# A gated-linear-attention block with a convolutional feed-forward: the down projection's matmuls walk their columns in another order in each block product

## The chip, the cores and the metric

The kernel runs on one core of one Trainium2 chip. The metric is the device time of one execution in microseconds. The kernel before has a median of 2124.78 us over three runs (2121.08, 2124.78 and 2126.06).

## The reference

One transformer layer over 2048 tokens of width 1024 in float32: a token mixer (chunked gated linear attention with 4 heads), then a causal convolutional feed-forward. Each is modulated by a conditioning vector and closed with a residual and a layer norm. What the change touches is the last product of the feed-forward:

```python
def conv_ffn(h, w_up, conv_w, conv_b, w_down):
    u, g = jnp.split(h @ w_up, 2, axis=-1)
    u = lax.conv_general_dilated(u, conv_w[:, None, :], window_strides=(1,), padding=((CONV_W - 1, 0),), ...) + conv_b
    return (jax.nn.silu(u) * g) @ w_down

def post_norm_residual(x, cs, w_mod, b_mod, ln_gain, ln_bias, sublayer):
    shift, scale, gate = jnp.split((cs @ w_mod + b_mod)[:, None, :], 3, axis=-1)
    y = sublayer(x * (1 + scale) + shift)
    return layer_norm(DN_ALPHA * x + (1 + gate) * y, ln_gain, ln_bias)
```

The hidden width is 2816, so the down projection is (2048 x 2816) times (2816 x 1024).

## The kernel before, in words

**The large products.** A float32 product is made of three matmuls in a reduced float32 format. Each operand is split into a high part (a cast on ScalarE, L104) and a low part (what the cast lost, a subtraction on VectorE, L107). `mm3` (L109 to L112) then issues high by high, high by low and low by high, all into the same PSUM bank. The first operand is the stationary one, 128 x 128, loaded as weights; the second is the moving one, 128 partitions by 512 columns, and the sums of those 512 columns fill one bank of 512 float32 columns.

**The down projection (L1833 to the end).** It uses a scheme with seven block products instead of eight (Strassen-Winograd), on each half of the tokens, p = 0 and 1 (1024 tokens each). The seven combinations of hidden blocks lie in DRAM as `hc_d[p][i]`, the seven of weight blocks as `wc_d[i]`; each has NP = 11 slices of 128 rows. `ORDER = (0, 1, 4, 5, 6, 3, 2)` is the order in which the products i run. This makes 14 block products; the text numbers them 1 to 14 in order of time, so product 1 is p = 0, i = 0, and product 14 is p = 1, i = 2.

One product takes 4 tiles t of 128 tokens, and for each tile 11 slices: `mms(t, gi, got)` (L1953) calls `mm3` once or twice, because `groups` pairs the slices. The stationary operand is a 128-column piece of the hidden combination, the moving one a 512-column slice `w[:, 0, o:o + 512]` (high) or `w[:, 1, o:o + 512]` (low) of the weight combination. So a product has 4 x 11 x 3 = 132 matmuls of 512 columns.

**Banks.** The eight PSUM banks are two sets of four: "A" (`ps_mm`) and "C" (`ps_w`), one bank per tile t. `INTO` (L1938) says which set a product adds to. Products i = 0, 1 and 4 are `fresh`: they begin new sums; the others add to what stands in the set. After each product `evict` (L1962) lets VectorE add the banks to the rows of the result in SBUF (L1965). ScalarE, VectorE and GpSimd then do the last layer norm of a tile (`ln2`, `ln2_last`), and SyncE's queue stores it. Product 14 goes tile by tile, so that the last layer norms spread out.

**Supply.** `d_load` (L1851) issues the transfers of two slices from DRAM on SyncE's queue, up to four groups ahead; `d_split` (L1862) makes the high and low parts up to three groups ahead, in tiles named `dhl` or, every third time, `hl`. TensorE takes its matmuls in the order of the program; the scheduler of the language lets the first of them mix with the last products of the up projection.

Of the kernel before, what the change touches and what calls it, by code (L numbers as in the profile page):

```python
# [16 lines left out]
P = 128  # L17
# [21 lines left out]
def kernel(  # L39
# [43 lines left out]
    def psum(tag, bufs=1):  # L83
        return ps.tile([P, 512], F32, tag=tag, name="ps_" + tag, bufs=bufs)
# [24 lines left out]
    def mm3(po, a, b, first, last, resumed=False):  # L109
        nc.tensor.matmul(po, a[0], b[0], start=first, stop=False, skip_group_check=resumed)  # L110
        nc.tensor.matmul(po, a[0], b[1], start=False, stop=False, skip_group_check=resumed)  # L111
        return nc.tensor.matmul(po, a[1], b[0], start=False, stop=last, skip_group_check=resumed)  # L112
# [341 lines left out]
    if True:  # L454
# [86 lines left out]
        for n, (dk, more) in enumerate(PE_ROWS):  # L541
            wk = mod_row(start[0][0], dk)
            for c in range(4):
                i = nc.tensor.matmul(pm0[:, c:c + 1], wk[:, c // 2, c % 2 * P:c % 2 * P + P], cs[:, dk:dk + 1],
                                     start=n == 0 and c == 0, stop=False, skip_group_check=True)
# [1287 lines left out]
    ORDER = (0, 1, 4, 5, 6, 3, 2)  # L1833
# [11 lines left out]
        return hs  # L1845

    groups = [(p, i, g) for p in range(2) for i in ORDER for g in range(0, NP, 2)]
    flip = [0]
    dloaded, dready = [], []

# [23 lines left out]
    def d_get(q):  # L1874
        while len(dloaded) < min(q + 4, len(groups)):
            d_load()
        while len(dready) < min(q + 3, len(groups)):
            d_split()
        return dready[q]
# [12 lines left out]
    def ln2_last(p, b, t):  # L1892
        a, sm = acc.pop((p, b, t))
        st = sts.pop()
        nc.vector.bn_stats(st[:, 1], a[:, 512:1024])
        mv = smp.tile([P, 2], F32, tag="mv", name="mv")
        nc.vector.bn_aggr(mv, st)

        rs = smp.tile([P, 2], F32, tag="rs", name="rs")
        nc.scalar.activation(rs[:, 1:2], mv[:, 1:2], AF.Sqrt, bias=eps[:, 0:1])  # L1900
        ys = []
        for half in range(2):
            cs_ = slice(half * 512, half * 512 + 512)
            y = t2p.tile([P, 512], F32, tag="t2", name="y")
            i = nc.vector.scalar_tensor_tensor(y, a[:, cs_], mv[:, 0:1], rows[2][half], op0=ALU.subtract, op1=ALU.mult)
            if half == 0:
                order(nc.vector.reciprocal(rs[:, 0:1], rs[:, 1:2]), i)
            cut = (0, 256, 512) if t == 3 and half == 1 else (0, 512)
            for c0, c1 in zip(cut, cut[1:]):
                nc.vector.scalar_tensor_tensor(y[:, c0:c1], y[:, c0:c1], rs[:, 0:1], rows[3][half][:, c0:c1],  # L1910
                                               op0=ALU.mult, op1=ALU.add)
                store(outr[p * 8 + b * 4 + t][:, half * 512 + c0:half * 512 + c1], y[:, c0:c1])
# [31 lines left out]
    for p in range(2):  # L1944
        bank = {"A": [None] * 4, "C": [None] * 4}
        for i in ORDER:
            kind, b, half, whole = INTO[i]
            cs_ = slice(half * 512, half * 512 + 512)
            fresh = i in (0, 1, 4)
            ng = (NP + 1) // 2  # L1950
            outer = p == 1 and i == ORDER[-1]

            def mms(t, gi, got):  # L1953
                n = min(2, NP - 2 * gi)
                h, w = got
                for k in range(n):
                    o = k * 512
                    mm3(bank[kind][t], (h[:, 0, o + t * P:o + t * P + P], h[:, 1, o + t * P:o + t * P + P]),
                        (w[:, 0, o:o + 512], w[:, 1, o:o + 512]),
                        fresh and gi == 0 and k == 0, gi == ng - 1 and k == n - 1, not fresh)  # L1960

            def evict(t):  # L1962
                a, sm = acc[p, b, t]
                acc_out = {"accum_out": sm[:, half:half + 1]} if whole and not outer else {}
                nc.vector.scalar_tensor_tensor(a[:, cs_], bank[kind][t], 1.0, a[:, cs_],  # L1965
                                               op0=ALU.mult, op1=ALU.add, **acc_out)
                if outer:
                    ln2_last(p, b, t)
                elif i in (3, 2):
                    work.append((ln2, p, b, t))  # L1970

            if fresh:
                bank[kind] = [psum("mm" if kind == "A" else "w", 4) for t in range(4)]
            if i == 3 and p == 0:
                work += [(init_acc, 1, 0, t) for t in range(4)]
            if outer:
                nc.vector.memset(eps, EPS)
                got = [d_get(q + gi) for gi in range(ng)]
                for t in range(4):
                    sts.append(smp.tile([P, 2, 6], F32, tag="bst", name="bst"))  # L1980
                    nc.vector.bn_stats(sts[-1][:, 0], acc[p, b, t][0][:, 0:512])
                    for gi in range(ng):
                        mms(t, gi, got[gi])
                        if gi % 3 == 1 and work:
                            f, *a_ = work.pop(0)
                            f(*a_)
                    evict(t)
            else:
                for gi in range(ng):
                    got = d_get(q + gi)  # L1990
                    if work and (gi > 0 or work[0][0] is init_acc):
                        f, *a_ = work.pop(0)
                        f(*a_)
                    for t in range(4):
                        mms(t, gi, got)
                        if gi == ng - 1:
                            evict(t)
            q += ng
        work += [(init_acc, 1, 1, t) for t in range(4)] if p == 0 else []
# [58 lines left out]
```

## Time and profile before

| what | value |
|---|---|
| median of three runs | 2124.78 us |
| the profiled execution | 2121.6 us |
| its span, first to last instruction | 2119.9 us |
| mean granted TensorE clock | 0.996 |
| TensorE matmuls | 9381, 2085.8 us busy |
| ScalarE and VectorE busy | 1003.4 us and 1529.5 us |
| moved by DMA | 546.24 MB |

How to read it: the rows of the profile are times of one execution. PE is TensorE's matmul row, PEld its weight loads, DVE VectorE, ACT ScalarE, POOL GpSimd, SP SyncE. Matmuls are pipelined, and the length that is recorded for one reaches into the next, so the distance from start to start tells its price. A row of a group gives line, engine, operation, tiles (out<-in), shapes and count, then the busy time in us and the mean ns of one, then the idle time of the engine just before and what ended it. A row of a wait reads: who waited, for whom, us in total, times, the longest.

### The profile page before, as it was taken

The numbers are of one execution on the slowest core, as the hardware profiler recorded it, in microseconds if no ns is written. First come the engines' busy times: TensorE is split into PE (matmuls) and PEld (weight loads), VectorE is DVE, ScalarE is ACT, GpSimd is POOL, SyncE is SP. The second block draws the span as 40 slices with busy tenths as digits, with TensorE's granted clock in tenths as the row PEclk, the third lists the DMA queues.
The fourth block names the chain that finished last, engine by engine and source line by source line (L and its number), as shares of the span: only waits on it lengthen the run. The fifth ranks groups of instructions, "written<-read, shape, count | busy, mean of one in ns | idle before, by whom it ended". The sixth has DMA issues, their size and how long they took to land.

```text
span 2119.9 us, 26188 instructions
## 1 busy us (share of the span) xinstructions
PE 2085.8 (98%) x9381; PEld 1721.9 (81%) x9381; DVE 1529.5 (72%) x2022; ACT 1003.4 (47%) x1405; POOL 107.0 (5%) x254
## 2 busy tenths in 40 slices
PE   9999999999999998999999999999999999999998
PEld 7887887778888787888888888888888888888886
DVE  6855757776687667878777787666676796577557
ACT  4648636674555544644444454333333443344332
POOL 0000000001112201100000000000000000020001
PEclk9999999999999999999999999999999999999999
DMA  9787888788745885777756679877777897677562
GB/s 336 304 295 261 283 306 286 268 306 317 277 145 196 310 289 192 274 249 285 273 194 219 219 253 321 288 258 273 246 276 256 295 325 250 206 247 251 189 200 89
DMA packets 192035, 546.24 MB, mean 258 GB/s; under 512 B 24928, under 2 KB 33504, under 8 KB 186272
## 3 DMA queue, kind: packets, MB, share of 16 engines
q1 hardware_dynamic: 191904, 544.56, 73.5%
q8 instruction: 74, 1.21, 0.2%
q14 instruction: 57, 0.47, 0.1%
HBM read 357.58 MB, written 186.91 MB: 257 GB/s over the span
## 4 chain that ended last, share of the span: by engine, by line
PE 71%; DVE 3%; ACT 2%; DMA 2%; issue 1%; POOL 1%; SPq 0%; DVEq 0%; POOLq 0%; ACTq 0%
PE ps_mm L110 15%; PE ps_mm L112 15%; PE ps_mm L111 15%; PE ps_w L111 7%; PE ps_w L110 7%; PE ps_w L112 7%; PE ps_w L1326 1%; PE ps_w L1354 1%; PE ps_w L1356 1%; PE ps_w L1310 1%; DMA hl<-wf_d 1%; DMA A<-a_d 0%; PE ps_w L1375 0%; PE ps_w L1416 0%; ACT on L1369 0%
## 5 line engine op out<-in xcount | busy, mean ns | idle before, releaser
L110 PE MATMUL ps_mm<-xc,hl 128*128 128x512 f32 x920 | 361.8, 393 | 6.2 <-ACT u L448 4.5
L111 PE MATMUL ps_mm<-xc,hl 128*128 128x512 f32 x920 | 359.5, 391 | 0.0
L112 PE MATMUL ps_mm<-xc,hl 128*128 128x512 f32 x920 | 358.8, 391 | 0.0
L110 PEld LDWEIGHTS ps_mm<-xc,hl 128*128 128x128 f32 x920 | 173.5, 189 | 46.4 <-ACT u L448 6.6
L112 PEld LDWEIGHTS ps_mm<-xc,hl 128*128 128x128 f32 x920 | 173.4, 189 | 36.5 <-DVE hl L107 0.2
L111 PEld LDWEIGHTS ps_mm<-xc,hl 128*128 128x128 f32 x920 | 173.6, 189 | 36.1 <-issue 0.5
L110 PE MATMUL ps_w<-xc,hl 128*128 128x512 f32 x464 | 180.6, 389 | 0.0
L111 PE MATMUL ps_w<-xc,hl 128*128 128x512 f32 x464 | 180.5, 389 | 0.0
L112 PE MATMUL ps_w<-xc,hl 128*128 128x512 f32 x464 | 180.5, 389 | 0.0
L1655 DVE SCALAR_TENSOR_TENSOR ct<-U,cw_sb,ct 128x512 f32<-128x512 f32 x176 | 131.8, 749 | 22.8 <-ACT ct L1649 20.2
L104 ACT CAST hl<-wu 128x1024 fp32r<-128x1024 f32 x90 | 94.8, 1053 | 104.1 <-PE ps_mm L112 76.9
L448 ACT COPY u<-ps_mm 128x512 f32<-128x512 f32 x112 | 65.3, 583 | 159.4 <-PE ps_mm L112 152.0
L104 ACT CAST dhl<-raw 128x1024 fp32r<-128x1024 f32 x57 | 60.1, 1054 | 159.2 <-PE ps_mm L112 98.5
L107 DVE TENSOR_TENSOR hl<-wu,hl 128x1024 fp32r<-128x1024 f32 x90 | 110.0, 1222 | 30.2 <-ACT hl L104 29.9
L107 DVE TENSOR_TENSOR dhl<-raw,dhl 128x1024 fp32r<-128x1024 f32 x57 | 69.7, 1223 | 65.4 <-ACT dhl L104 65.4
L107 DVE TENSOR_TENSOR hl<-raw,hl 128x1024 fp32r<-128x1024 f32 (+1 forms) x63 | 69.3, 1104 | 56.1 <-ACT hl L104 55.8
L110 PE MATMUL ps_mm<-hl,xg 128*128 128x512 f32 x240 | 104.0, 433 | 3.6 <-DVE z L1526 3.6
L104 ACT CAST hl<-raw 128x1024 fp32r<-128x1024 f32 (+1 forms) x63 | 60.0, 955 | 99.4 <-PE ps_mm L112 42.1
L104 ACT CAST hl<-wg 128x1024 fp32r<-128x1024 f32 x56 | 59.0, 1053 | 97.6 <-PE ps_mm L112 85.0
L110 PE MATMUL ps_mm<-dhl 128*128 128x512 f32 x264 | 102.7, 389 | 0.0
L111 PE MATMUL ps_mm<-dhl 128*128 128x512 f32 x264 | 102.7, 389 | 0.0
L112 PE MATMUL ps_mm<-dhl 128*128 128x512 f32 x264 | 102.7, 389 | 0.0
(284 smaller groups left out, 4743.7 us busy)
## 6 DMA issues: line engine op xcount, KB each, us to landing
hc_d<-ct SPq DMA_DIRECT2D x154, 256.0 KB, 2.9
raw<-hc_d SPq DMA_DIRECT2D x70, 512.0 KB, 4.2
draw<-wc_d SPq DMA_DIRECT2D x70, 512.0 KB, 4.6
wu<-in_wup_dram SPq DMA_DIRECT2D x44, 512.0 KB, 5.3
wg<-in_wup_dram SPq DMA_DIRECT2D x44, 512.0 KB, 4.3
wh_d<-hl SPq DMA_DIRECT2D x22, 1024.0 KB, 4.8
hl<-wh_d SPq DMA_DIRECT2D x22, 1024.0 KB, 6.6
mraw<-in_mws_dram SPq DMA_DIRECT2D x40, 512.0 KB, 6.0
```

Of the source, the lines that this page charges most:

```text
L104: accs["copy"] = nc.scalar.copy(h, src)
L107: return nc.vector.tensor_tensor(l, src if lsrc is None else lsrc, h.bitcast(F32), op=ALU.subtract)
L110: nc.tensor.matmul(po, a[0], b[0], start=first, stop=False, skip_group_check=resumed)
L111: nc.tensor.matmul(po, a[0], b[1], start=False, stop=False, skip_group_check=resumed)
L112: return nc.tensor.matmul(po, a[1], b[0], start=False, stop=last, skip_group_check=resumed)
L448: return t, nc.scalar.copy(t, po)
L1310: nc.tensor.matmul(pav[:, i], KI[:, s * P:s * P + P], Q[:, s], start=True, stop=True)
L1326: nc.tensor.matmul(pst[:, s % 2 * DV:s % 2 * DV + DV], KTt[:, s * P:s * P + P], v[s], start=True, stop=True)
L1354: nc.tensor.matmul(pos_, at[:, i], v[s], start=True, stop=st is None)
L1356: nc.tensor.matmul(pos_, Q[:, s, 0:128], st, start=False, stop=True)
L1655: nc.vector.scalar_tensor_tensor(ct, U[:, o + i:o + i + 512], cw_sb[:, j, i:i + 1], ct, op0=ALU.mult, op1=ALU.add)
```

## The change

A table `WALK` gives each of the 14 block products an order in which its matmuls go through their 512 columns. An entry is (rows, run, down). With run = 0 the columns go from 0 to 511, or with down = 1 from 511 to 0. Otherwise the 512 columns are seen as `rows` equal parts, each cut into runs of `run` columns, and the walk takes the first run of each part, then the second of each part, and so on (with down = 1 from the last run to the first); inside a run the columns rise. The view is made once for the moving operand and once for the bank, so column c of the weights still ends in column c of the bank. The stationary operand, the evictions and the number of columns are unchanged; products 1 and 14 keep the order of before.

| product | p, i | columns |
|---|---|---|
| 1 and 14 | 0, 0 and 1, 2 | as before |
| 2 | 0, 1 | all 512 backwards |
| 3, 4 | 0, 4 and 0, 5 | 2 parts, runs of 16; 4 from the last run down |
| 5 | 0, 6 | 2 parts, runs of 32 |
| 6 | 0, 3 | 4 parts, runs of 16 |
| 7 | 0, 2 | runs of 16 from the last to the first |
| 8, 9, 10 | 1, 0, then 1, 1, then 1, 4 | 2 parts, runs of 8; of 64; of 4 |
| 11 | 1, 5 | 8 parts, runs of 16 |
| 12, 13 | 1, 6 and 1, 3 | 4 parts, runs of 32 and of 16, both down |

```diff
@@ -1845,6 +1845,8 @@
     groups = [(p, i, g) for p in range(2) for i in ORDER for g in range(0, NP, 2)]
+    WALK = ((1, 0, 0), (1, 0, 1), (2, 16, 0), (2, 16, 1), (2, 32, 0), (4, 16, 0), (1, 16, 1),
+            (2, 8, 0), (2, 64, 0), (2, 4, 0), (8, 16, 0), (4, 32, 1), (4, 16, 1), (1, 0, 0))
     flip = [0]
@@ -1947,6 +1949,15 @@
             fresh = i in (0, 1, 4)
+            rows_of, run, down = WALK[p * 7 + ORDER.index(i)]
+
+            def walk(a):
+                if run == 0:
+                    return a[:, ::-1] if down else a
+                v = a.rearrange("p (r c e) -> p c r e", r=rows_of, e=run)
+                v = v[:, ::-1] if down else v
+                return v[:, :, 0] if rows_of == 1 else v
+
             ng = (NP + 1) // 2
@@ -1955,8 +1966,8 @@
                 for k in range(n):
                     o = k * 512
-                    mm3(bank[kind][t], (h[:, 0, o + t * P:o + t * P + P], h[:, 1, o + t * P:o + t * P + P]),
-                        (w[:, 0, o:o + 512], w[:, 1, o:o + 512]),
+                    mm3(walk(bank[kind][t]), (h[:, 0, o + t * P:o + t * P + P], h[:, 1, o + t * P:o + t * P + P]),
+                        (walk(w[:, 0, o:o + 512]), walk(w[:, 1, o:o + 512])),
                         fresh and gi == 0 and k == 0, gi == ng - 1 and k == n - 1, not fresh)
```

## The prediction

> **What bounds the kernel now.** I read the page first, for which engine is full and which engine the chain that ended last runs through.
>
> ```profile
> span 2119.9 us, 26188 instructions
> ...
> PE 2085.8 (98%) x9381; PEld 1721.9 (81%) x9381; DVE 1529.5 (72%) x2022; ACT 1003.4 (47%) x1405; POOL 107.0 (5%) x254
> ...
> PE   9999999999999998999999999999999999999998
> ...
> PEclk9999999999999999999999999999999999999999
> ...
> PE 71%; DVE 3%; ACT 2%; DMA 2%; issue 1%; POOL 1%; SPq 0%; DVEq 0%; POOLq 0%; ACTq 0%
> ```
>
> TensorE is full in every slice, at a granted clock of nine tenths or more throughout, and the chain runs through it. A busy PE is not a PE at its peak, so next I cut out the down projection by time (busy time of each engine by stretch) and looked at its matmuls one by one (the timeline of PE; two rows of 28, without a break between them).
>
> ```profile
> core 0: us, PE busy (x) PEld busy (x) DVE busy (x) ACT busy (x) POOL busy (x), PEclk, DMA share, GB/s
> 1687.50:2111.50 424.00, 424.00 (x1872) 350.95 (x1871) 297.69 (x365) 167.60 (x191) 30.48 (x48) 1.00 0.67 225
> 2111.50:2119.90 8.40, 0.54 (x3) 0.12 (x1) 4.53 (x9) 0.29 (x1) 0.00 (x0) 0.72 0.24 90
> ```
>
> ```profile
> 1799.76 0.39 PE L110 MATMUL ps_mm<-dhl 128*128 128x512 f32 x1
> ...
> 1805.88 0.39 PE L110 MATMUL ps_mm<-dhl 128*128 128x512 f32 x1
> ```
>
> PE is busy for all 424.00 us of that stage, at clock 1.00. A matmul lasts 0.39 us in the record, but the next one starts sooner: 27 starts lie between the two rows, and (1805.88 - 1799.76) / 27 = 226.7 ns from start to start. That is the price of one matmul of 512 columns here, 226.7 / 512 = 0.443 ns a column; the 389 ns overlap with the neighbours. Check: 1872 x 226.7 ns = 424.4 us, the length of the stage. Nothing else sets the pace: weight loads, VectorE and ScalarE have room, and in the waits of this stage it is they who wait for PE:
>
> ```profile
> ACT dhl L104 <- PE ps_mm L112: 98.0, 29, 4.3
> ...
> ACT dhl L104 <- PE ps_w L112: 56.8, 17, 4.3
> ```
>
> So in this stage PE's own rate is the time. After it come 8.4 us of layer norm and stores, which the change does not touch.
>
> **How much the change reaches.** The groups of matmuls of this stage, one of three equal lines (L110; L111 and L112 have the same counts):
>
> ```profile
> L110 PE MATMUL ps_mm<-dhl 128*128 128x512 f32 x264 | 102.7, 389 | 0.0
> ...
> L110 PE MATMUL ps_w<-dhl 128*128 128x512 f32 x192 | 74.7, 389 | 0.0
> ...
> L110 PE MATMUL ps_mm<-hl 128*128 128x512 f32 x88 | 34.2, 389 | 0.0
> ...
> L110 PE MATMUL ps_w<-hl 128*128 128x512 f32 x72 | 28.0, 389 | 0.0
> ```
>
> 3 x (264 + 192 + 88 + 72) = 1848 matmuls, 132 for each of 14 block products, or 132 x 226.7 ns = 29.9 us a product. WALK leaves the first and the last product as they were; 12 x 132 = 1584 matmuls get another order. Product 2 (p = 0, i = 1) runs all 512 columns backwards. The other eleven walk forwards inside runs of 4 to 64 columns and jump between runs.
>
> What moves in the program: on PE, where the second product ends and the third (p = 0, i = 4) begins, before and then after. dhl and hl are the split operands, ps_w the bank.
>
> ```order
> L111 MATMUL ps_w<-hl 128x512
> L112 MATMUL ps_w<-hl 128x512
> L110 MATMUL ps_w<-dhl 128x512
> L111 MATMUL ps_w<-dhl 128x512
> L112 MATMUL ps_w<-dhl 128x512
> ```
>
> ```order
> L111 MATMUL ps_w<-hl 128x512
> L112 MATMUL ps_w<-hl 128x512
> L110 MATMUL ps_w<-dhl 128x16x2x16
> L111 MATMUL ps_w<-dhl 128x16x2x16
> L112 MATMUL ps_w<-dhl 128x16x2x16
> ```
>
> The same instructions in the same places; only the shape of the pattern differs: 16 steps, at each 2 runs of 16 columns. The backward product above it has one dimension as before, so its rows read alike. VectorE, ScalarE, GpSimd and SyncE keep every instruction and transfer in its place. One thing is added. On PE, where product 8 (p = 1, i = 0) begins, with the semaphores that each row waits for, before and then after:
>
> ```order
> L112 MATMUL ps_w<-hl 128x512
> L110 MATMUL ps_mm<-dhl 128x512 [waits Activation_49]
> L111 MATMUL ps_mm<-dhl 128x512 [waits DVE_49]
> L112 MATMUL ps_mm<-dhl 128x512
> L110 MATMUL ps_mm<-dhl 128x512
> ```
>
> ```order
> L112 MATMUL ps_w<-hl 128x32x16
> L110 MATMUL ps_mm<-dhl 128x32x2x8 [waits PE_49,Activation_49]
> L111 MATMUL ps_mm<-dhl 128x32x2x8 [waits DVE_49]
> L112 MATMUL ps_mm<-dhl 128x32x2x8
> L110 MATMUL ps_mm<-dhl 128x32x2x8
> ```
>
> The first matmul into each of the four banks waits for PE's own semaphore as well, in product 8 and again in product 9: eight waits.
>
> **The eight waits.** Each is for the earlier matmuls into the same bank. Those of product 8 wrote in product 6, those of product 9 in product 7, so a whole product (29.9 us) lies between and the wait is over before it starts: 0. Behind such a wait stands all of PE, and the casts of ScalarE behind that. Were each to hold PE until the matmul just before it has ended, it would cost what now overlaps, 389 - 227 = 162 ns, and eight of them 1.3 us. I take 0 and keep 1.3 us for the range.
>
> **The 1584 matmuls.** Nothing hides a slower matmul here, since PE has no idle time; each ns on all of them is 1.6 us of the end, in full. No matmul of this trace walks its columns in another order, so the price is bounded by the nearest rows.
>
> From above: there is a matmul that takes 512 columns at about half the pace, the plain-float32 one at L296, and one of 256 columns, L1326 (the chain of waits: start, length, what; then the groups by shape).
>
> ```profile
> 515.33 1.73 PE ps_w L1326 x8
> ...
> 1267.00 1.72 PE ps_w L296 x4
> ```
>
> ```profile
> L1326 PE MATMUL ps_w<-v,KTt 128*128 128x256 f32 x120 | 29.9, 379 | 0.0
> ...
> L296 PE MATMUL ps_w<-G,ones 128*128 128x512 f32 x8 | 3.8, 602 | 0.0
> ```
>
> 1.72 / 4 = 430 ns for 512 columns, 1.73 / 8 = 216 ns for 256. So half pace costs 430 - 227 = 203 ns more a matmul.
>
> From below: those two rows give (430 - 216) / 256 = 0.836 ns a column and 2 ns fixed. If our matmuls stream exactly twice as fast, 512 columns need 214 + 2 = 216 ns, and at most 11 ns a matmul could be won: 1584 x 11 ns = 17 us.
>
> What do broken patterns cost elsewhere? Row L562 casts and L565 subtracts 384 columns that are written in 24 runs of 16 with gaps between; the unbroken casts and subtractions of 512 and 1024 stand beside them (one tile's instructions; groups by shape).
>
> ```profile
> L562 ACT CAST waw<-war x1: 494/494/494, 20.1 to 20.1; 128x384 fp32r<-128x384 f32 x1
> L565 DVE TENSOR_TENSOR waw<-war,waw x1: 549/549/549, 25.3 to 25.3; 128x384 fp32r<-128x384 f32 x1
> ```
>
> ```profile
> L104 ACT CAST hl<-wu 128x1024 fp32r<-128x1024 f32 x90 | 94.8, 1053 | 104.1 <-PE ps_mm L112 76.9 <-DVE wu L352 12.0 <-PE ps_w L112 7.4
> ...
> L104 ACT CAST h<-s 128x512 fp32r<-128x512 f32 x34 | 20.8, 612 | 5.3 <-PE ps_mm L112 2.9 <-DVE s L352 2.5
> ```
>
> ```profile
> L107 DVE TENSOR_TENSOR hl<-wu,hl 128x1024 fp32r<-128x1024 f32 x90 | 110.0, 1222 | 30.2 <-ACT hl L104 29.9
> ...
> L107 DVE TENSOR_TENSOR h<-s,h 128x512 fp32r<-128x512 f32 x34 | 23.3, 686 | 13.4 <-ACT h L104 13.4
> ```
>
> ScalarE: (1053 - 612) / 512 = 0.861 ns a column, so 384 unbroken ones would take 612 - 128 x 0.861 = 502 ns; the broken ones took 494. VectorE: 1.047 ns a column, 686 - 134 = 552 ns; 549 measured. Twenty-four breaks cost nothing. Weakness: these engines move a column in 0.86 to 1.05 ns, PE in 0.44, so a break that fits under their pace may not fit under PE's. Still, the addresses come from the same kind of pattern, no row charges for a break, and I take 0 for PE too.
>
> The Trainium skill speaks on both sides. The Trainium skill's page "PSUM — Partial Sum Buffer", Specifications (TRN2), says of PSUM's 8-byte lines that any non-contiguous pattern slows matmuls significantly; by that sentence all 12 products lose, and with 203 ns each the sum would be 2443.2 us. The Trainium skill's page "Advanced Engine Details and Errata", Memory Cachelines, puts it as every two consecutive elements being contiguous for best throughput, and the two of a float32 pair stay neighbours in all fourteen orders, the backward one too; by that the sum stays. No row here shows a broken matmul, so neither is tested yet.
>
> The sum: 0 for 1584 matmuls, 0 for eight waits, nothing removed. The profiled execution took 2121.6 us (span 2119.9 and 1.7 around it), so 2121.6 stays; the median of the three runs is 2124.8, 3.2 above, and the runs lie from 2121.1 to 2126.1. I predict the median, 2124.8. About 0.2%, 4.2 us, is what a measurement of this kernel can tell from no change.
>
> **The rivals.** Each price is added to 2124.8.
>
> 1. Slower: only going backwards costs. If PE fetches or writes columns in pairs, rising ones, product 2 falls to half pace while runs of 4 or more keep theirs. 132 x 203 ns = 26.8 us: 2151.6. For it: 0.443 ns a column against 0.836 shows that the fast pace is twice another one that this PE has, so something could switch. Against it: nothing in the trace depends on direction. It decides the sign from 4.2 / 132 = 32 ns a matmul on.
> 2. Slower: each jump costs. The eleven broken products make 413 jumps for one matmul each (31 for each of the six with runs of 16, 15 for each of the two with 32, 63 with 8, 7 with 64, 127 with 4), 132 x 413 = 54,516 in all. At one column's time, 0.443 ns, 24.1 us: 2148.9; at two, 2173.1. Against it: the broken rows of ScalarE and VectorE.
> 3. Slower: every changed order runs at half pace. 1584 x 203 ns = 321.6 us: 2446.4. For it: no cover anywhere. Against it: the same rows. The rule of the Trainium skill's page "PSUM — Partial Sum Buffer" (Specifications) is this case; no row here shows it.
> 4. Faster: the remainder of 11 ns goes, at most 17 us: 2107.8. Nothing in the trace ties it to the order of columns.
>
> That the change does less than it says (a pattern folded back into a plain one) cannot be for the eleven, whose shapes stand in the order; for the backward one it would give the forecast's time.
>
> **How the numbers follow.** No effect: 0.64. Backwards alone: 0.14. Jumps: 0.07. Half pace throughout: 0.11. Faster: 0.04. So faster 0.04, within 0.2% 0.64, slower 0.32. The likeliest case alone spans 2119 to 2130, from the spread of the runs and the 1.3 us of waits. To hold 8 in 10 the range goes up to backwards alone with the spread above it, 2155, which takes in half of the jumps too (0.64 + 0.14 + 0.03); half pace and the dear jumps stay outside.
>
> **What would show it.** In the timeline of PE after the change: product 2 starts at 1722.9 us, as the first matmul into ps_w from dhl does now,
>
> ```profile
> L110 PE MATMUL ps_w<-dhl x192: 389/389/389, 1722.9 to 2110.5; 128*128 128x512 f32 x192
> ```
>
> and then one product each 29.9 us. Right: 226.7 ns from start to start in every product, and the stage still 424 us. Wrong: product 2 alone at some 430 ns (rival 1), the excess growing with the jumps and greatest in product 10 with runs of 4 (rival 2), 430 ns in twelve products (rival 3), or idle time at the start of products 8 and 9 (the waits).

## The result: 12.75 us slower

| | before | after |
|---|---|---|
| median of three runs | 2124.78 us | 2137.53 us |
| their lowest and highest | 2121.08 and 2126.06 | 2136.89 and 2138.75 |
| span of the profiled execution | 2119.9 us | 2135.7 us |
| stage of the down projection | 424.00 us | 440.80 us |

The ratio is 1.0060, with a 95% interval of 1.0039 to 1.0081: 8 to 17 us slower. That is inside the range, but it isn't the case that was called likeliest (no effect). The spans of the profiled executions differ by more, 15.8 us, because the one of before ran 3.2 us under its median. The page of the kernel after:

```profile
span 2135.7 us, 26190 instructions
...
PE 2105.2 (99%) x9381; PEld 1727.1 (81%) x9381; DVE 1530.1 (72%) x2022; ACT 1002.7 (47%) x1405; POOL 107.4 (5%) x254
...
PEclk9999999999999999999999999999999999999999
```

The counts of matmuls, casts and subtractions are those of before, and so is the clock. PE is busy 19.4 us longer and its weight loads 5.2; the other engines stay within 0.7. The two stretches that the prediction cut out (busy time by stretch, same columns):

```profile
core 0: us, PE busy (x) PEld busy (x) DVE busy (x) ACT busy (x) POOL busy (x), PEclk, DMA share, GB/s
1686.90:2127.70 440.80, 440.80 (x1873) 352.86 (x1871) 298.50 (x365) 167.66 (x191) 30.50 (x48) 1.00 0.64 217
2127.70:2135.70 8.00, 0.21 (x1) 0.00 (x0) 4.52 (x9) 0.29 (x1) 0.00 (x0) 0.75 0.19 69
```

The stage is 16.8 us longer and PE is busy for all of it at clock 1.00. It began 0.6 us earlier and the tail is 0.4 us shorter, which leaves the 15.8 us of the span. So the time came from matmuls that follow each other more slowly, not from a wait or a throttled clock. The first matmul of products 2 to 14 and the last one of product 14, from the timeline of PE (start, length, then the instruction):

```profile
1722.36 0.40 PE L110 MATMUL ps_w<-dhl 128*128 128x512 f32 x1
1753.16 0.41 PE L110 MATMUL ps_w<-dhl 128*128 128x512 f32 x1
1784.85 0.40 PE L110 MATMUL ps_mm<-dhl 128*128 128x512 f32 x1
1815.65 0.40 PE L110 MATMUL ps_mm<-dhl 128*128 128x512 f32 x1
1846.88 0.40 PE L110 MATMUL ps_mm<-dhl 128*128 128x512 f32 x1
1877.42 0.40 PE L110 MATMUL ps_w<-dhl 128*128 128x512 f32 x1
1908.22 0.41 PE L110 MATMUL ps_mm<-dhl 128*128 128x512 f32 x1
1940.34 0.40 PE L110 MATMUL ps_w<-dhl 128*128 128x512 f32 x1
1970.29 0.41 PE L110 MATMUL ps_w<-dhl 128*128 128x512 f32 x1
2003.30 0.41 PE L110 MATMUL ps_mm<-dhl 128*128 128x512 f32 x1
2034.92 0.40 PE L110 MATMUL ps_mm<-dhl 128*128 128x512 f32 x1
2066.16 0.40 PE L110 MATMUL ps_mm<-dhl 128*128 128x512 f32 x1
2097.79 0.39 PE L110 MATMUL ps_w<-dhl 128*128 128x512 f32 x1
...
2127.52 0.39 PE L112 MATMUL ps_w<-hl 128*128 128x512 f32 x1
```

The distance of two neighbouring rows divided by 132 (131 for product 14) is the pace of a product, the mean distance from one start to the next. In the table, a jump is a step from the end of one run to a run that isn't its neighbour above, and the excess is over the 226.7 ns of before.

| product | order | ns a matmul | excess, ns | jumps | excess per jump, ns |
|---|---|---|---|---|---|
| 2 | all backwards | 233.3 | 6.7 | none | |
| 3 | 2 parts, runs of 16 | 240.0 | 13.3 | 31 | 0.43 |
| 4 | the same, down | 233.3 | 6.7 | 31 | 0.22 |
| 5 | 2 parts, runs of 32 | 236.6 | 9.9 | 15 | 0.66 |
| 6 | 4 parts, runs of 16 | 231.3 | 4.6 | 31 | 0.15 |
| 7 | runs of 16, down | 233.3 | 6.7 | 31 | 0.22 |
| 8 | 2 parts, runs of 8 | 243.3 | 16.6 | 63 | 0.26 |
| 9 | 2 parts, runs of 64 | 226.9 | 0.2 | 7 | 0.03 |
| 10 | 2 parts, runs of 4 | 250.1 | 23.4 | 127 | 0.18 |
| 11 | 8 parts, runs of 16 | 239.5 | 12.8 | 31 | 0.41 |
| 12 | 4 parts, runs of 32, down | 236.7 | 10.0 | 15 | 0.67 |
| 13 | 4 parts, runs of 16, down | 239.6 | 12.9 | 31 | 0.42 |
| 14 | as before | 227.0 | 0.3 | none | |

The excesses of products 2 to 13 sum to 123.8 ns, times 132 is 16.3 us. From the first start to the last the down projection took 16.4 us more (1686.93 to 2127.52 us now, 1687.48 to 2111.66 before), so this is the whole of what it lost. No product is at half pace, the backward one lost 3% and not 90%, and the price per jump differs by a factor of twenty. Within a product the distances repeat while the traffic of DMA and VectorE changes (product 10 alternates 254 and 246 ns throughout), so the walk sets the pace and not a neighbour on the chip.

The eight waits, at the place where product 8 begins (timeline of PE, the last matmul of product 7 and the first of product 8):

```profile
1907.99 0.40 PE L112 MATMUL ps_w<-hl 128*128 128x512 f32 x1
1908.22 0.41 PE L110 MATMUL ps_mm<-dhl 128*128 128x512 f32 x1
```

Product 8 starts 230 ns after the last matmul of product 7, whose own pace is 233: the wait on PE's semaphore cost nothing. At the other seven places too PE has no idle time.

### The profile page after: what moved, and what is told of

It is laid out like the page before. It is cut to its first block, busy times and chain, and to the rows that moved or that the text cites. A ratio compares the mean times of both kernels' runs of the same rounds, so it can differ in the third digit from the quotient of the medians.

```text
span 2135.7 us, 26190 instructions
## 1 busy us (share of the span) xinstructions
PE 2105.2 (99%) x9381; PEld 1727.1 (81%) x9381; DVE 1530.1 (72%) x2022; ACT 1002.7 (47%) x1405; POOL 107.4 (5%) x254
## 4 chain that ended last, share of the span: by engine, by line
PE 73%; DVE 2%; ACT 2%; DMA 1%; issue 1%; POOL 1%; DVEq 0%; SPq 0%; POOLq 0%; ACTq 0%
PE ps_mm L110 16%; PE ps_mm L111 16%; PE ps_mm L112 16%; PE ps_w L112 7%; PE ps_w L111 7%; PE ps_w L110 7%; PE ps_w L1326 1%; PE ps_w L1354 1%; PE ps_w L1310 1%; PE ps_w L1356 1%; DMA hl<-wf_d 1%; PE ps_w L1416 1%; PE ps_w L1375 1%; ACT on L1369 0%; ACT sq L1366 0%
## 5 line engine op out<-in xcount | busy, mean ns | idle before, releaser
L111 PE MATMUL ps_mm<-dhl 128*128 128x512 f32 x264 | 105.4, 399 | 0.0
L112 PE MATMUL ps_mm<-dhl 128*128 128x512 f32 x264 | 105.2, 399 | 0.0
L110 PE MATMUL ps_mm<-dhl 128*128 128x512 f32 x264 | 104.7, 397 | 0.0
```

## The experiments

The theory after the result: a matmul is slower because TensorE reads its moving operand from SBUF in another order, and the price depends on which addresses follow each other. Rivals: the price lies in writing the sums to PSUM in another order; or it is a price per jump, wherever the jump leads; or the reads compete with the weight loads that run beside the matmuls, so that smaller weight loads make room.

**Reading or writing.** Each kernel keeps one of the two walks. `read_only`:

```diff
-                    mm3(walk(bank[kind][t]), (h[:, 0, o + t * P:o + t * P + P], h[:, 1, o + t * P:o + t * P + P]),
+                    mm3(bank[kind][t], (h[:, 0, o + t * P:o + t * P + P], h[:, 1, o + t * P:o + t * P + P]),
```

> Only the moving operand is walked; the bank takes its sums in plain order, so columns of the result change places in twelve of the fourteen products. Theory R (the cost of a walk lies where TensorE reads the moving columns out of SBUF): the starts in products 2 to 13 lie as far apart as in the changed kernel (233, 240, 233, 237, 231, 233, 243, 227, 250, 240, 237, 240 ns) and the time is about 2137 us. Theory W (it lies where the sums are written into PSUM): 226.7 ns in every product, time about 2125 us.

Measured: 2139.28 us beside 2124.31 for the kernel before, a ratio of 1.0075 (1.0049 to 1.0101). Product 10, from its first matmul to that of product 11 (timeline of PE):

```profile
1974.82 0.41 PE L110 MATMUL ps_w<-dhl 128*128 128x512 f32 x1
2007.83 0.41 PE L110 MATMUL ps_mm<-dhl 128*128 128x512 f32 x1
```

33.01 us / 132 = 250.1 ns, as in the changed kernel, and the other products agree with the table to 0.1 ns. `write_only`:

```diff
-                        (walk(w[:, 0, o:o + 512]), walk(w[:, 1, o:o + 512])),
+                        (w[:, 0, o:o + 512], w[:, 1, o:o + 512]),
```

> Only the bank is walked; the moving operand is read in plain order, so columns of the result change places in twelve of the fourteen products. Theory W: products 2 to 13 as in the changed kernel (231 to 250 ns except product 9), time about 2137 us. Theory R: 226.7 ns in every product, time about 2125 us.

Measured: 2123.62 us, ratio 1.0002 (0.9984 to 1.0020). Products 2 and 10, each with the start of the next one:

```profile
1731.36 0.39 PE L110 MATMUL ps_w<-dhl 128*128 128x512 f32 x1
1761.28 0.39 PE L110 MATMUL ps_w<-dhl 128*128 128x512 f32 x1
...
1970.72 0.39 PE L110 MATMUL ps_w<-dhl 128*128 128x512 f32 x1
2000.64 0.39 PE L110 MATMUL ps_mm<-dhl 128*128 128x512 f32 x1
```

29.92 us / 132 = 226.7 ns in both, backwards or in runs of 4. So reading the moving operand from SBUF carries the whole price and writing the bank none; the other ten products ran at 226.7 ns as well. The Trainium skill's page "PSUM — Partial Sum Buffer", Specifications (TRN2), has any non-contiguous pattern slow matmuls significantly; for the eleven broken patterns of this kernel, written to PSUM, the measurement disagrees: 226.7 ns for each.

**The length of the runs and the place in the program.** `scan_runs` puts other walks into the table, some of them those of the changed kernel in other products.

```diff
-    WALK = ((1, 0, 0), (1, 0, 1), (2, 16, 0), (2, 16, 1), (2, 32, 0), (4, 16, 0), (1, 16, 1),
-            (2, 8, 0), (2, 64, 0), (2, 4, 0), (8, 16, 0), (4, 32, 1), (4, 16, 1), (1, 0, 0))
+    WALK = ((2, 128, 0), (2, 64, 0), (2, 32, 0), (2, 16, 0), (2, 8, 0), (2, 4, 0), (2, 2, 0),
+            (8, 2, 0), (8, 4, 0), (8, 16, 0), (8, 32, 0), (32, 4, 0), (1, 0, 0), (1, 0, 0))
```

> Other walks, both sides: two parts with runs of 128, 64, 32, 16, 8, 4 and 2 in products 1 to 7, then eight parts with runs of 2, 4, 16 and 32 and 32 parts with runs of 4 in products 8 to 12; 13 and 14 plain. If a jump has one price, the excess over 226.7 ns doubles with each halving of the run: from 0.4 ns a jump at runs of 16 (13 ns) to 27, 55 and 109 ns at 8, 4 and 2. If the walk only shifts when a conflict falls, as the changed kernel's 0, 10, 13, 17 and 23 ns for runs of 64 to 4 suggest, the same figures come back in their new places and runs of 2 cost some 25 to 35 ns. If a pair has to stay together, runs of 2 are still no cliff; a cliff would be 200 ns.

Measured: 2189.22 us in one run. By product, for product 1 without its start, where other matmuls mix in: 226.7, 226.7, 236.6, 240.0, 243.3, 250.2, 339.9, 487.7, 278.4, 239.5, 236.6, 223.3, 226.9 and 226.7 ns. The starts of products 7, 8 and 9, and of 12 and 13:

```profile
1881.24 0.51 PE L110 MATMUL ps_w<-dhl 128*128 128x512 f32 x1
1926.11 0.73 PE L110 MATMUL ps_mm<-dhl 128*128 128x512 f32 x1
1990.49 0.48 PE L110 MATMUL ps_w<-dhl 128*128 128x512 f32 x1
...
2090.08 0.39 PE L110 MATMUL ps_mm<-dhl 128*128 128x512 f32 x1
2119.56 0.39 PE L110 MATMUL ps_mm<-dhl 128*128 128x512 f32 x1
```

Three things follow. The six walks that the changed kernel also has, 2 parts with runs of 64 to 4 and 8 parts with runs of 16, cost the same within 0.2 ns in another product, four of them in the other set of banks. Runs of 2 columns are a cliff: 44.87 / 132 = 339.9 ns in 2 parts and 64.38 / 132 = 487.7 ns in 8. And one walk, 32 parts with runs of 4, is faster than the plain order: 29.48 / 132 = 223.3 ns. The Trainium skill's page "SBUF — State Buffer", Specifications (TRN2), asks for at least two hits on a 16-byte line for full bandwidth; runs of 2 float32 columns have two, yet they took 339.9 and 487.7 ns, so for TensorE's reads here two hits weren't enough. Runs of 4 have four and took 223.3 to 278.4 ns, so the length of the run isn't all of it either.

**The distance of the jumps.** `scan_lines` keeps runs of 4 columns (16 bytes) in several products and varies only the number of parts, hence the distance from one run to the next.

```diff
...
+    WALK = ((64, 4, 0), (16, 4, 0), (4, 4, 0), (32, 4, 0), (32, 4, 1), (64, 4, 1), (16, 8, 0),
+            (32, 8, 0), (8, 8, 0), (4, 8, 0), (16, 16, 0), (1, 4, 1), (1, 64, 1), (1, 0, 0))
```

> Other walks, both sides, runs of 4 (one 16-byte line) at different distances: 64, 16, 4, 32 parts, then 32 and 64 parts from the last run down, runs of 8 with 16, 32, 8 and 4 parts, 16 parts with runs of 16, then runs of 4 and of 64 from the last to the first. Known: runs of 4 with 2 parts 250 ns, 8 parts 278, 32 parts 223.4. Theory RJ: each jump has a price, so all walks with runs of 4 and 127 jumps cost alike, some 250 ns, which the 223.4 already contradicts. Theory RB (lines that lie a multiple of 256 bytes apart are in one bank, and successive reads of one bank stall): 4 parts (512 bytes apart) 260 to 280 ns, 16 and 64 parts (128 and 32 bytes apart) about as plain, 220 to 232; runs of 64 backwards 227.

Measured: 2137.99 us in one run; 231.1 (product 1, again without its start), 246.5, 267.9, 226.7, 226.8, 231.4, 230.7, 232.5, 258.7, 231.2, 240.0, 233.4, 226.8 and 226.7 ns. The starts of products 2 to 5 (16, 4 and 32 parts), and of 12 and 13 (runs of 4 in one part, from the last to the first):

```profile
1721.83 0.40 PE L110 MATMUL ps_w<-dhl 128*128 128x512 f32 x1
1754.37 0.43 PE L110 MATMUL ps_w<-dhl 128*128 128x512 f32 x1
1789.73 0.40 PE L110 MATMUL ps_mm<-dhl 128*128 128x512 f32 x1
1819.65 0.39 PE L110 MATMUL ps_mm<-dhl 128*128 128x512 f32 x1
...
2037.63 0.40 PE L110 MATMUL ps_mm<-dhl 128*128 128x512 f32 x1
2068.43 0.40 PE L110 MATMUL ps_mm<-dhl 128*128 128x512 f32 x1
```

The upward walks with runs of 4 all make 127 jumps, and with the rows of `scan_runs` and of the changed kernel they cost, by the distance from the start of one run to the start of the next part's: 1024 bytes +23 ns, 512 bytes +41, 256 bytes +52, 128 bytes +20, 64 bytes 0 or -3, 32 bytes +5. One price per jump is refuted. So it is by the walks downwards in one part: all 512 columns singly (product 2 of the changed kernel), runs of 16 (its product 7) and runs of 4 (product 12 here, 30.80 / 132) all took 233.3 ns, with 511, 31 and 127 steps back. The three distances that are multiples of 256 bytes have 64, 96 and 112 forward steps among the 127 jumps, which makes 0.37, 0.43 and 0.46 ns for each, about the time of one column (0.443 ns); 128 bytes, with 120 forward steps, cost 0.17 ns for each.

`distances_384` asks whether that holds where the parts are other distances apart: 384 columns instead of 512, in the bank, the moving operand and the eviction.

```diff
...
+    WALK = ((1, 0, 0), (2, 4, 0), (3, 4, 0), (4, 4, 0), (6, 4, 0), (8, 4, 0), (12, 4, 0),
+            (16, 4, 0), (24, 4, 0), (32, 4, 0), (48, 4, 0), (6, 8, 0), (4, 8, 0), (1, 0, 0))
...
-                    mm3(walk(bank[kind][t]), (...), (walk(w[:, 0, o:o + 512]), walk(w[:, 1, o:o + 512])),
+                    mm3(walk(bank[kind][t][:, 0:384]), (...), (walk(w[:, 0, o:o + 384]), walk(w[:, 1, o:o + 384])),
...
```

> Only 384 of the 512 columns of each product are computed and evicted (a quarter of the result lacks the down projection), so that the parts can lie at distances that are no power of two. Runs of 4 with 2, 3, 4, 6, 8, 12, 16, 24, 32 and 48 parts in products 2 to 11 (48, 32, 24, 16, 12, 8, 6, 4, 3 and 2 lines of 16 bytes apart), runs of 8 with 6 and 4 parts in 12 and 13 (16 and 24 lines apart), plain in 1 and 14; every walk with runs of 4 makes 95 jumps. Plain 173 ns. Theory RJ (one price a jump): products 2 to 11 alike. Theory RB (successive lines a multiple of 256 bytes apart meet in one bank and cost about one TensorE cycle, 0.42 ns, each): 2, 3 and 6 parts (48, 64 and 80 such steps) 20, 27 and 33 ns over plain, 4, 8, 16, 24, 32 and 48 parts within some 7 ns of plain, 12 parts (128 bytes apart) in between.

Measured: 2047.29 us in one run, plain products 173.3 ns. The multiples of 256 bytes again cost (768 bytes +18 ns, without two steps of 0.5 and 1.9 us in which product 2 waited for its operands; 512 bytes +20, 256 bytes +31: 0.37, 0.31 and 0.38 ns for each forward step), and 384, 192 and 64 bytes little or nothing (+3, +2, -2.5), 128 bytes +9. But 16 parts, 96 bytes apart, had not been expected to cost: products 8 and 9 start at

```profile
1866.91 0.40 PE L110 MATMUL ps_mm<-dhl 128*128 128x384 f32 x1
1896.82 0.35 PE L110 MATMUL ps_w<-dhl 128*128 128x384 f32 x1
```

29.91 / 132 = 226.6 ns, 53 more than plain. And 6 parts with runs of 8, 256 bytes apart, cost nothing (173.9), where 8 parts with runs of 8 at 512 columns, 256 bytes apart too, cost +32. "Multiples of 256 bytes" is thus a good description of runs of 4 and no full rule. To see whether the 96 bytes were an accident of that product, `distances_again` put that walk into three products and others twice:

```diff
...
+    WALK = ((1, 0, 0), (16, 4, 0), (6, 8, 0), (16, 4, 0), (2, 4, 0), (6, 8, 0), (24, 4, 0),
+            (16, 4, 0), (3, 4, 0), (6, 8, 0), (24, 4, 0), (3, 4, 0), (12, 4, 0), (1, 0, 0))
```

> 384 of 512 columns as in the run with distances, with some of its walks at two or three places: 16 parts with runs of 4 in products 2, 4 and 8, 6 parts with runs of 8 in 3, 6 and 10, 24 parts with runs of 4 in 7 and 11, 3 parts with runs of 4 in 9 and 12, 2 parts in 5, 12 parts in 13. If the price belongs to the walk: 227, 173 to 174, 171, 193, 191 and 183 ns at each place. If it belongs to the steady pattern that the stream falls into from where it was: the same walk differs from place to place by 3 ns or more, and 16 parts fall below 190 ns somewhere.

Measured: 2060.82 us in one run; products 4 and 8 start, and the next ones after them,

```profile
1772.99 0.40 PE L110 MATMUL ps_mm<-dhl 128*128 128x384 f32 x1
1802.92 0.36 PE L110 MATMUL ps_mm<-dhl 128*128 128x384 f32 x1
...
1873.59 0.40 PE L110 MATMUL ps_mm<-dhl 128*128 128x384 f32 x1
1903.50 0.37 PE L110 MATMUL ps_w<-dhl 128*128 128x384 f32 x1
```

29.93 and 29.91 us: 226.7 ns, and in the third place, product 2, as well, apart from two single steps of 0.5 and 1.1 us, the second at a wait for its operands. Runs of 8 in 6 parts gave 173.5 in all three places, 24 parts 170.7 and 3 parts 193.4 in both. The price belongs to the walk and not to the place, with two exceptions that took two steady paces: 12 parts (182.7 here before, 186.6 now), and 32 parts at 512 columns (223.3 and 226.7).

**Long runs.** If only near neighbours count, runs that fill blocks of 256 bytes (64 columns) should be free in any order, downwards too.

```diff
...
+    WALK = ((1, 0, 0), (1, 64, 1), (2, 64, 0), (2, 64, 1), (2, 128, 0), (4, 64, 0), (1, 128, 1),
+            (2, 64, 0), (4, 64, 1), (1, 64, 1), (2, 128, 1), (2, 64, 1), (4, 64, 0), (1, 0, 0))
```

> The changed kernel with other walks in products 2 to 13: runs of 64 and 128 columns alone (256 and 512 bytes), with 1, 2 and 4 parts, up and down; result as the reference's. If a walk is free as long as every run fills whole blocks of 256 bytes (theory RB: the next run begins in the bank that the plain order would have come to): 226.7 ns in each product and the time of the kernel before, 2125 us within 4. If a jump or going down has a price of its own: the products with (1, 64, 1) and (2, 64, 1) lie 3 to 7 ns higher and the time is 2128 to 2135 us.

Measured: 2121.81 us beside 2122.46, ratio 0.9997 (0.9988 to 1.0007). The first matmuls of products 2 and 14:

```profile
1719.63 0.39 PE L110 MATMUL ps_w<-dhl 128*128 128x512 f32 x1
...
2078.67 0.39 PE L110 MATMUL ps_w<-dhl 128*128 128x512 f32 x1
```

359.04 us / (12 x 132) = 226.7 ns. The same kind of change, twelve reordered products with the same added waits, is free when the runs have 64 columns or more.

**The weight loads.** They read SBUF beside the matmuls; a load of 128 columns lasts 188 ns in the record, and one comes every 227. If matmul and weight load shared one supply, smaller loads should give time back. `half_weights` gives the second of each three matmuls 64 stationary columns, `thin_weights` gives 32 to all but the first and the last of each tile's chain; the sums of the columns left out are missing.

```diff
...
+                    nc.tensor.matmul(walk(po), h[:, 0, a:a + P], wh, start=first, stop=False, skip_group_check=not fresh)
+                    nc.tensor.matmul(walk(po[0:64]), h[:, 0, a:c], wl, start=False, stop=False, skip_group_check=not fresh)
+                    nc.tensor.matmul(walk(po), h[:, 1, a:a + P], wh, start=False, stop=last, skip_group_check=not fresh)
```

> The changed kernel, but the second of three matmuls (high by low) has 64 stationary columns instead of 128, so half the tokens of each tile miss that term. Theory R with weights (moving columns and the weights of the next matmul are read through the same door, 32 of 544 cycles in the plain products being the weights): while the short weights load, the matmul that runs is shorter; plain products fall from 226.7 to about 224.5 ns on average (one of three at 220), and the excess of walked ones falls too. If weights have no part: 226.7 ns in products 1 and 14, and 231 to 250 in the others as before.

Measured: 2141.0 us in one run. The plain product 14 went up, to 229.9 ns; products 3 and 2 stayed (240.0, 233.4), product 10 fell only to 248.9, but product 6 went from 231.3 to 229.4 and product 13 from 239.6 to 233.5.

```diff
...
+                    for part, mv, full in ((0, wh, first), (0, wl, False), (1, wh, last)):
+                        m, a = P if full else 32, o + t * P
+                        nc.tensor.matmul(walk(bank[kind][t][0:m]), h[:, part, a:a + m], mv, start=fresh and first and full,
+                                         stop=last and part == 1, skip_group_check=not fresh)
```

> The changed kernel, but all matmuls of a tile's chain except its first and last have 32 stationary columns instead of 128, so most of the product is left out for 96 of 128 tokens. Theory RW (the moving columns are read side by side with the weights of the next matmul, and what is lost depends on how the two fall together): with a quarter of the weights the plain products 1 and 14 fall from 226.7 towards 216 ns, and the excess of the walked ones shrinks to a few ns. Theory RJ (the read of the moving columns alone pays for its jumps, whatever the weights do): products 1 and 14 stay at 226.7 ns, and the others lie as far above them as in the changed kernel (5 to 23 ns).

Measured: 2140.27 us in one run. Product 14, the first matmul and the first of its last three, with 129 steps between them (timeline of PE):

```profile
2099.94 0.40 PE L1973 MATMUL ps_w<-dhl 128*128 128x512 f32 x1
...
2129.79 0.86 PE L1973 MATMUL ps_w<-hl 128*32 128x512 f32 x3
```

29.85 / 129 = 231.4 ns, while the weight loads beside it (groups by shape, from 2069 to 2130 us) were much shorter than 188 ns:

```profile
L1973 PEld LDWEIGHTS ps_w<-dhl 128*32 128x32 f32 x92 | 10.0, 109 | 11.0
```

Less weight to load made a plain matmul 4.7 ns slower, not faster, while the walked products stayed or fell: product 3 at 240.0, product 10 at 246.7, product 4 at 228.8, which is less than plain here. Over the plain pace of the same kernel product 3 kept 8.6 of its 13.3 ns and product 10 kept 15.3 of 23.4. That the excess is simply what the weights take falls with the sign of the plain product; that weights and walk act on each other doesn't, since the excess over plain went down with the weights. `weights_apart` then left the moving operand plain and laid the stationary columns apart, with a step of 1, 2 or 4 columns by product; the rows of the result change places.

```diff
+            step = (1, 2, 4)[(p * 7 + ORDER.index(i)) // 2 % 3]
-                    mm3(bank[kind][t], (h[:, 0, o + t * P:o + t * P + P], h[:, 1, o + t * P:o + t * P + P]),
+                    at = slice(o + t // step * step * P + t % step, o + t // step * step * P + t % step + step * (P - 1) + 1, step)
+                    mm3(bank[kind][t], (h[:, 0, at], h[:, 1, at]),
```

> The kernel before, with plain walks; the stationary tile takes every column (products 1, 2, 7, 8, 13, 14), every second (3, 4, 9, 10) or every fourth (5, 6, 11, 12) of the same 512 tokens, so its 128 columns lie in 32, 64 or 128 lines of 16 bytes, and rows of the result belong to other tokens. Theory RW: more lines of weights take more from the moving columns: 226.7 ns with step 1, about 235 to 240 with step 2, about 250 to 270 with step 4. Theory RJ: 226.7 ns in all products.

Measured: 2133.62 us in one run. The starts of products 3 and 4 (step 2), and of 5 and 6 (step 4):

```profile
1756.91 0.39 PE L110 MATMUL ps_w<-dhl 128*128 128x512 f32 x1
1787.71 0.39 PE L110 MATMUL ps_mm<-dhl 128*128 128x512 f32 x1
1818.51 0.40 PE L110 MATMUL ps_mm<-dhl 128*128 128x512 f32 x1
1849.53 0.40 PE L110 MATMUL ps_mm<-dhl 128*128 128x512 f32 x1
```

```profile
L112 PEld LDWEIGHTS ps_mm<-dhl 128*128 128x128 f32 x64 | 19.8, 310 | 0.0
```

233.3 ns at step 2, 235.0 at step 4, where a weight load took 310 ns instead of 188 (the row is of the stretch of products 5 and 6), and 226.7 at step 1. Neither rival's number came: the expectation of 235 to 240 and 250 to 270 ns was too high, and the one that the weights don't matter was wrong. The order in which the weights are read does reach the pace of the matmuls, by 3 to 4%. A row of 310 ns isn't the price of a load: loads start 235 ns apart there, so the records of neighbouring loads overlap, as those of matmuls do. How the two reads meet stays open.

**A version that beats both kernels.** `all_32x4` gives all fourteen products the walk that ran at 223 ns.

```diff
...
+    WALK = ((32, 4, 0), (32, 4, 0), (32, 4, 0), (32, 4, 0), (32, 4, 0), (32, 4, 0), (32, 4, 0),
+            (32, 4, 0), (32, 4, 0), (32, 4, 0), (32, 4, 0), (32, 4, 0), (32, 4, 0), (32, 4, 0))
```

> The changed kernel with one walk in all fourteen products, 32 parts with runs of 4, which took 223.4 ns in one profile and 226.7 in another against 226.7 for the plain order; result as the reference's. If 223.4 holds: 1848 x 3.3 ns = 6.1 us faster than the kernel before, 2119 us. If the walk falls into several steady patterns from product to product, the products lie between 223 and 227 ns and the time between 2119 and 2125 us; no change that can be measured.

Measured: 2117.95 us beside 2122.46 for the kernel before, ratio 0.9980 (0.9969 to 0.9990). The stage (busy time by stretch), and then the first matmuls of products 2 and 14:

```profile
1689.70:2107.90 418.20, 418.20 (x1873) 350.10 (x1871) 298.36 (x365) 167.24 (x191) 30.48 (x48) 1.00 0.68 228
```

```profile
1724.68 0.38 PE L110 MATMUL ps_w<-dhl 128*128 128x512 f32 x1
...
2078.43 0.38 PE L110 MATMUL ps_w<-dhl 128*128 128x512 f32 x1
```

353.75 us / 1584 = 223.3 ns in every product, and a stage of 418.2 us instead of 424.0: 1848 x 3.4 ns = 6.3 us less by the pace, 4.5 us (2 to 7) by the medians. `mm3_32x4` puts the same walk into `mm3` itself, for all of the kernel's products of that kind:

```diff
+    def walk(v):
+        return v.rearrange("p (r c e) -> p c r e", r=32, e=4)
+
+        po, b = walk(po), [walk(b[0]), walk(b[1])]
```

> The kernel before with the walk of 32 parts and runs of 4 made inside mm3, so that all 8256 of its matmuls (the other projections too) read and write their 512 columns in that order; result as the reference's. If the 3.3 ns a matmul belong to the walk wherever PE sets the pace: 8256 x 3.3 ns = 27 us faster than the kernel before, about 2095 us. If they hang on the down projection alone (its tiles, its neighbours): 2116 to 2119 us. If the steady pattern is lost at every change to another kind of matmul: 2119 to 2125 us.

Measured: 2115.53 us beside 2122.36, ratio 0.9968 (0.9949 to 0.9987). That is faster than before by 7 us (3 to 11), but far from what 3.4 ns on every matmul would give: the down projection ran at 223.3 ns, in the earlier phases the steps vary between 220 and 240 ns with a mean of 226.4 to 227 (227.2 in the kernel before). The faster steady pace isn't reached there, and why isn't known. The two intervals overlap, so the second step over `all_32x4` isn't shown.

## Why the prediction was right or wrong, point by point

- **What bounds the stage** was right. PE has no idle time, so all of the 16.3 us that the matmuls lost came out at the end: 15.8 us of span, after a start of the stage that lay 0.6 us earlier.
- **The eight waits at 0** were right; product 8 begins at the pace of product 7.
- **The 1584 matmuls at 0** was the step that failed, where it took the free breaks of ScalarE and VectorE for PE as well ("no row charges for a break, and I take 0 for PE too"). The two don't carry over. VectorE's subtraction at L565 reads one operand in runs of 16, most of them 128 bytes apart, and took 549 ns for a computed 552; 16 parts with runs of 16, also 128 bytes apart, cost PE 13.3 ns a matmul (`scan_lines`, 240.0). Whether that is due to the slower pace of those engines, the weakness named in the same place (0.86 to 1.05 ns a column and PE 0.44), no run shows. What PE's order costs was measured from -3.4 to +261 ns a matmul, here 10.3 ns on average (123.8 / 12).
- **The range** held the result mostly by luck. Its top, 2155, was set for product 2 at half pace, 26.8 us; product 2 lost 0.9 us, and the other 15.5 us came from the eleven products that this case left at 0. That those pay at all was in the cases of the jumps (chance 0.07) and of half pace throughout (0.11, outside the range).
- **Rival 1** had the direction right for product 2 and the price wrong: +6.7 ns for 203. And it isn't backwards as such: blocks of 64 or 128 columns in falling order cost nothing, and blocks of 16 or 4 cost the same 6.7 ns as 512 single steps.
- **Rival 2** came nearest by its time (2148.9 for a measured 2137.53), its sign (the greatest excess in product 10) came, and its 54,516 jumps would fit the loss of products 3 to 13, 15.5 us, with 0.28 ns each. But it isn't the mechanism: the price per jump differed from 0.03 to 0.67 ns in the same kernel, and with the same number of jumps from less than 0 to 52 ns a matmul by the number of parts alone, which sets the distance.
- **Rival 3**, half pace everywhere, didn't occur; no product of the changed kernel lost more than 11%. Its sign was right and its place wrong: nothing was lost in writing PSUM.
- **Rival 4**, a gain, wasn't in this change. That the trace before ties nothing to the order of columns was true and no evidence against it: another order, 32 parts with runs of 4, wins 3.4 of the 11 ns.
- **What is shown and what is open.** Shown: the place (reading the moving operand), that the price changes with the length of the runs and the distance of the parts, that it belongs to the walk with two exceptions, and that the size and the layout of the weights have an effect too. Open: whether it arises in the memory or in what makes the addresses; the rule for all distances (96 bytes apart dear, runs of 8 at 256 bytes once dear and once free), why less weight to load makes the plain pace slower, and what sets the two steady paces of one walk.

## What to carry to other kernels

Where TensorE is the bound, the order in which it reads its moving operand is part of the price. By these runs: keep runs of at least 64 float32 columns, avoid runs of 2, and put a needed permutation on the side of PSUM, where the twelve orders of this change were free. A pattern that is free on one engine need not be free on another, nor one that is free to write be free to read; measure the pace from start to start in the block that uses it.

## What the runs showed of the hardware that had not been expected

- The plain order isn't the fastest for 512 columns: runs of 4 columns taken 64 bytes apart gave 223.3 ns against 226.7.
- At 384 columns runs of 4 taken 96 bytes apart cost 53 ns on 173, the same in three places, although 64 bytes (-2.5 ns) and 128 bytes (+9) on either side are cheap.
- With 32 instead of 128 stationary columns a weight load took 109 ns instead of 188, and the matmul beside it 231.4 instead of 226.7.
